# A 31-tap channelwise convolution: one channel tile on TensorE through diagonal weights, or two through shifted copies made by way of DRAM

## The chip, the core and the metric

The kernel runs on one core of a Trainium2 chip. The metric is the time that the device takes for one execution, in microseconds (us), lower being better. TensorE (PE in the profile), VectorE (DVE), ScalarE (ACT) and GpSimd (POOL) compute; SyncE (SP) only issues DMAs.

## The reference, cut to what matters

Two layers of a decoder trunk on 256 tokens of 1024 features, in float32. Layer 0 is attention of two kinds and a gated feed-forward; layer 1 is a gated MLP (mixer C) beside a convolution (mixer D), and a second feed-forward. The change lies in mixer D:

```python
proj = h @ w_in + b_in
gz, ca, cg = jnp.split(proj, [2 * GMLP_WIDTH, 2 * GMLP_WIDTH + CONV_CH], axis=-1)
gu, gv = jnp.split(jax.nn.gelu(gz), 2, axis=-1)
... # mixer C: layer norm of gv, a causal 128 x 128 product per group, times gu
c = ca * jax.nn.sigmoid(cg)
c = lax.conv_general_dilated(c, conv_w[:, None, :], window_strides=(1,), padding=[(CONV_KERNEL - 1, 0)],
                             dimension_numbers=('NWC', 'WIO', 'NWC'), feature_group_count=CONV_CH) + conv_b
d_out = jax.nn.silu(layer_norm(c, cln_g, cln_b))
return jnp.concatenate([c_out, d_out], axis=-1) @ w_out
```

`c` has 512 channels and 256 tokens. Each channel has 31 weights of its own, and its output at token s is the sum over t of weight t times the input at s + t - 30.

## The kernel before

Activations lie with channels on the partitions: 512 channels are four tiles (`ct` 0 to 3) of 128. Every large product is made of float32r parts: weights and activations are split into a high and a low part, and three products (`passes`, L225 to L227, high-high, high-low, low-high) give one of nearly float32 accuracy. Weights come in blocks of 1 MB on SP's queue (`Block.load`, L116) into a ring of three buffers `raw`. ScalarE makes each half's high part `whi` (L133), and VectorE, or GpSimd for some blocks, the low part `wlo` (L137). When a block's second half is split, the load of the block three places on is issued, so that this load waits for that split. The order of TensorE is that of the code, and GpSimd's in this stage too; the other engines and SP are ordered by a scheduler when the program is built.

`tick` is called once or twice per group of products. It spreads two kinds of background work over the stage: splitting of later weight blocks (`pump`), and taps of the convolution on VectorE (`taps_along`, `TAP_RATE` taps per tick).

In layer 1 the stage around the change runs so on TensorE (L1137 to L1162): `gated(0)` makes channel tiles 0 and 1 of `c` into `cpad` (30 zeros ahead of 256 tokens), `gv_steps(1)`, `gated(1)` (tiles 2 and 3), `project_gu(0)`, 12 taps of tile 3, `project_gu(1)`, four products `spatial(p)` of mixer C with two taps behind each, and the last 11 taps. Tiles 0 to 2 are convolved on VectorE: a tap is one scalar_tensor_tensor (L1077, the first one L1075) over 128 channels and 256 tokens. Tile 3 is convolved on TensorE (`taps_pe`, L1056): each tap has a diagonal 128 x 128 matrix, high and low part, which ScalarE makes from the identity (`tap_diag`, L929, twelve of them while layer 0's feed-forward runs, 19 in this stage), and three products with the split tile `c_hi`, `c_lo`.

After that: `spatial(p)` (L1122) ends in a chain of ScalarE, GpSimd twice, ScalarE, GpSimd (L1131 to L1135) that writes part p of `oT_hi`, `oT_lo`. The output projection `out_steps` (L1207) begins with three steps of three products (`SOME[0]`): part 0 for both halves of the output columns, then part 1 for the first half. Then `mean` (L1170) sums the four convolved tiles over channels, and `center`, `scale`, `conv_out` make the layer norm and write parts 4 to 7. The rest is the residual, a norm, and layer 1's feed-forward (blocks `f1`, loaded from `in_ffn_w_in`).

Of the kernel before, what the change touches and what calls it, by code (L numbers as in the profile page):

```python
# [28 lines left out]
P = 128  # L29
# [7 lines left out]
EPS = 1e-6  # L37
NEG = -3.0e38
TAPS = 31


WRAW = 3
# [20 lines left out]
N_T1 = (10, 5, 10)  # L63


TAP_RATE = 0.55
N_DIAG = 12
SOME = (3, 4, 2, 4)
LAMBDA_INIT = 0.8 - 0.6 * math.exp(-0.3 * 0)

# [2 lines left out]
def trunk_kernel(ctx: ExitStack, tc: tile.TileContext, a: dict, out: bass.AP):  # L73
# [4 lines left out]
    wsplit = ctx.enter_context(tc.tile_pool(name="wsplit", bufs=8))  # L78
    act = ctx.enter_context(tc.tile_pool(name="act", bufs=1))
    small = ctx.enter_context(tc.tile_pool(name="small", bufs=3))  # L80
    pmm = ctx.enter_context(tc.tile_pool(name="pmm", bufs=4, space=bass.MemoryType.PSUM))

    def mm_bank():
# [195 lines left out]
    def col(name, i):  # L279
        return vec[:, rows[name] + i:rows[name] + i + 1]  # L280
# [62 lines left out]
    def run(steps):  # L343
        for _ in steps:
            pass
# [572 lines left out]
    wsT = mp.tile([P, NH, P], F32, name="wsT")  # L918
    biasT = mp.tile([P, 4, P], F32, name="biasT")
    cw = mp.tile([P, TAPS, 4], F32, name="cw")  # L920
    cw2 = mp.tile([P, 2, TAPS * 4], F32, name="cw2")
    bv = mp.tile([P, 512], F32, name="bv")
    ones = mp.tile([P, P], F32, name="ones")
    diag = mp.tile([P, N_DIAG, 2, P], FR, name="diag")

    def tap_diag(d, t, ct):

        for i in range(2):
            nc.scalar.activation(d[:, i, :], ident, AF.Copy, scale=cw2[:, i, t * 4 + ct:t * 4 + ct + 1])  # L929

    def odd_setup(ptag):

# [44 lines left out]
        nc.tensor.transpose(pt[:, :TAPS * 4], cw_rows[:TAPS * 4, :P], ident[:TAPS * 4, :TAPS * 4])  # L977
        cwf = cw.rearrange("p a b -> p (a b)")
        nc.vector.tensor_copy(cwf, pt[:, :TAPS * 4])
        hi = mp.tile([P, TAPS * 4], FR, name="cw_hi")  # L980
        nc.scalar.activation(hi, cwf, AF.Copy)
        nc.vector.tensor_copy(cw2[:, 0, :], hi.bitcast(F32))
        nc.vector.tensor_tensor(cw2[:, 1, :], cwf, hi.bitcast(F32), op=ALU.subtract)
        for t in range(N_DIAG):
            tap_diag(diag[:, t], t, 3)
        yield

    with tc.tile_pool(name="ffn0", bufs=1) as fp, tc.tile_pool(name="pf0", bufs=1, space=bass.MemoryType.PSUM) as pf:
# [12 lines left out]
    with tc.tile_pool(name="odd", bufs=1) as op, tc.tile_pool(name="pod", bufs=1, space=bass.MemoryType.PSUM) as pod:  # L1001
# [45 lines left out]

        follow(gv_steps(0), spare)

        cpad = op.tile([P, 4, S + TAPS - 1], F32, name="cpad")  # L1050
        nc.gpsimd.memset(cpad[:, :, :TAPS - 1], 0.0)
        conv = op.tile([P, 4, S], F32, name="conv")
        c_hi = op.tile([P, S + TAPS - 1], FR, name="c_hi")
        c_lo = op.tile([P, S + TAPS - 1], FR, name="c_lo")

        def taps_pe(ct):  # L1056

            ps = mm_bank()
            for t in range(TAPS):
                d = diag[:, t] if t < N_DIAG else diag2[:, t - N_DIAG]  # L1060
                passes(ps[:, :S], (d[:, 0, :], d[:, 1, :]), (c_hi[:, t:t + S], c_lo[:, t:t + S]), t == 0, t == TAPS - 1)
                if t < TAPS - 1:
                    yield
            nc.vector.tensor_scalar(conv[:, ct, :], ps[:, :S], col("conv_b", ct), None, op0=ALU.add)

        live, credit = deque(), [0.0]
# [24 lines left out]
        def gated(j):  # L1091
            wa, wg = blocks["ca", j], blocks["cg", j]
            for f in range(2):
                ps = mm_bank()
                project_T(ps, 0, wg, f)
                project_T(ps, 1, wa, f)
                ct = 2 * j + f
                sgm = scratch()[:, :S]
                with tc.high_priority(30):
                    sigmoid = nc.scalar.activation(sgm, ps[:, :S], AF.Sigmoid, bias=col("b_in", 12 + ct))  # L1100
                    nc.vector.scalar_tensor_tensor(cpad[:, ct, TAPS - 1:], ps[:, S:], col("b_in", 8 + ct), sgm,
                                                   op0=ALU.add, op1=ALU.mult)
                    if ct == 3:
                        split(c_hi, c_lo, cpad[:, ct, :])
                    else:
                        live.append((ct, 0))
            return sigmoid
# [28 lines left out]

        pool_order = in_order("Pool")  # L1137
        gated(0)
        diag2 = op.tile([P, TAPS - N_DIAG, 2, P], FR, name="diag2")
        for t in range(N_DIAG, TAPS):  # L1140
            tap_diag(diag2[:, t - N_DIAG], t, 3)
        run(gv_steps(1))
        last = gated(1)
        with tc.issue_after(last.ins):
            for m in range(MT):
                gv_stats(m)
        project_gu(0)
        taps = taps_pe(3)
        for _ in range(N_DIAG):
            next(taps)  # L1150
        for m in range(MT):
            gv_norm(m)
        last = project_gu(1)
        with tc.issue_after(last.ins):

            nc.scalar.activation(small.tile([P, 2], F32, name="st2")[:, 0:1], ident[:, 0:1], AF.Silu)
        for p in range(4):
            spatial(p)
            for _ in range(2):
                next(taps)  # L1160
        run(taps)
        while live:  # L1162
            tap_dve()
        background.clear()
# [3 lines left out]
        cm = [None] * MT  # L1168

        def mean():  # L1170
            for i, ct in enumerate((3, 0, 1, 2)):
                nc.tensor.matmul(pm[:, :S], ones, conv[:, ct, :], start=i == 0, stop=i == 3)

        def center(m):
# [125 lines left out]
```

## Time and profile before

| | |
|---|---|
| median of 3 runs | 631.92 us (630.7 to 632.24) |
| the profiled execution: its time, its span | 633.2 us, 631.4 us |
| TensorE busy, VectorE busy | 609.0 us (96%), 421.1 us (67%) |
| ScalarE busy, GpSimd busy | 345.7 us (55%), 121.7 us (19%) |
| mean granted TensorE clock | 0.989 of full speed |
| DMA | 104.32 MB, mean 165 GB/s |

The span runs from the first to the last instruction. A busy time sums over stages with different limits, so the stage of the convolution, about 355 to 412 us from the start, has to be read by itself: from windows, the engines' timelines and the chain of waits.

### The profile page before, as it was taken

How to read it: one execution, taken by the hardware profiler on the slowest of the kernel's cores; microseconds unless marked ns; L12 is line 12 of the kernel's file. 1: busy time of each engine (PE TensorE's matmuls, PEld its weight loads, DVE VectorE, ACT ScalarE, POOL GpSimd, SP SyncE). 2: the span in 40 equal slices, each digit the busy share in tenths (PEclk: the TensorE clock that was granted, in tenths of full speed). 3: DMA queues.
4: the chain of work that ended last, by engine and by line, in shares of the span. 5: the costliest groups of instructions: out<-in, count | busy, mean ns of one | idle time of the engine just before them, and what ended most of it. 6: DMA issues, size and time to landing. Idle time of an engine off the chain costs nothing.

```text
span 631.4 us, 8906 instructions
## 1 busy us (share of the span) xinstructions
PE 609.0 (96%) x3420; PEld 517.6 (82%) x3420; DVE 421.1 (67%) x710; ACT 345.7 (55%) x621; POOL 121.7 (19%) x97
## 2 busy tenths in 40 slices
PE   7989799999999999999998999988999999999997
PEld 5867577787988888888886899867988888888886
DVE  3799998547666648664446389986766666665431
ACT  5764686555655587553446775446455555554320
POOL 1998321101000000000003695550000000000000
PEclk9999799999999999999999799999999999999999
DMA  7855424224766437555552553225656555555401
GB/s 248 308 196 175 158 106 132 70 66 149 245 225 215 146 128 266 185 168 185 199 197 67 167 199 134 68 89 178 208 193 201 196 174 173 193 199 190 145 0 67
DMA packets 72791, 104.32 MB, mean 165 GB/s; under 512 B 3068, under 2 KB 56492, under 8 KB 72748
## 3 DMA queue, kind: packets, MB, share of 16 engines
q1 hardware_dynamic: 72748, 103.74, 49.5%
q8 instruction: 27, 0.44, 0.3%
q14 instruction: 16, 0.13, 0.1%
HBM read 102.69 MB, written 1.05 MB: 164 GB/s over the span
## 4 chain that ended last, share of the span: by engine, by line
PE 52%; issue 29%; DVE 11%; POOL 3%; ACT 2%; DMA 1%; SPq 1%; POOLq 0%; DVEq 0%; ACTq 0%
PE mm L233 15%; PE mm L225 8%; PE mm L227 8%; PE mm L234 8%; PE mm L226 8%; DVE wlo L137 3%; DVE scr L331 2%; PE tq L700 1%; DMA raw<-in_even_w_in 1%; POOL rm L310 1%; DVE t L627 1%; PE po L728 1%; ACT whi L133 1%; DVE t L621 1%; PE tq L718 1%
## 5 line engine op out<-in xcount | busy, mean ns | idle before, releaser
L133 ACT ACTIVATE whi<-raw 128x1024 fp32r<-128x1024 f32 (+1 forms) x192 | 197.7, 1040 | 175.7 <-PE mm L233 80.1
L137 DVE TENSOR_TENSOR wlo<-raw,whi 128x1024 fp32r<-128x1024 f32 (+1 forms) x166 | 206.3, 1248 | 124.5 <-ACT whi L133 122.9
L233 PE MATMUL mm<-xT,whi 128*128 128x512 f32 x640 | 226.8, 399 | 0.0
L234 PE MATMUL mm<-xT,wlo 128*128 128x256 f32 x640 | 179.7, 281 | 0.0
L233 PEld LDWEIGHTS mm<-xT,whi 128*128 128x128 f32 x640 | 120.2, 188 | 29.6 <-issue 0.2
L234 PEld LDWEIGHTS mm<-xT,wlo 128*128 128x128 f32 x640 | 120.9, 189 | 0.0
L225 PE MATMUL mm<-whi,xT 128*128 128x512 f32 (+1 forms) x176 | 68.2, 387 | 0.6 <-ACT xT L545 0.5
L137 POOL TENSOR_TENSOR wlo<-raw,whi 128x1024 fp32r<-128x1024 f32 (+1 forms) x26 | 62.9, 2439 | 19.7 <-ACT whi L133 19.6
L227 PE MATMUL mm<-whi,hT_lo 128*128 128x512 f32 (+1 forms) x176 | 66.5, 378 | 0.0
L226 PE MATMUL mm<-wlo,hT_hi 128*128 128x512 f32 (+1 forms) x176 | 66.5, 378 | 0.0
L225 PE MATMUL mm<-whi,hT_hi 128*128 128x512 f32 (+1 forms) x176 | 66.4, 378 | 0.0
L227 PE MATMUL mm<-whi,xT 128*128 128x512 f32 (+1 forms) x176 | 64.1, 364 | 1.1 <-DVE xT L240 1.1
L226 PE MATMUL mm<-wlo,xT 128*128 128x512 f32 (+1 forms) x176 | 64.3, 366 | 0.5 <-DVE wlo L137 0.5
L310 POOL TENSOR_TENSOR rm<-st,neg_half 128x1 f32<-128x1 f32 x8 | 7.1, 894 | 188.9 <-DVE st L308 188.9
L225 PEld LDWEIGHTS mm<-whi,xT 128*128 128x128 f32 x176 | 34.5, 196 | 7.8 <-issue 1.6
L227 PEld LDWEIGHTS mm<-whi,xT 128*128 128x128 f32 x176 | 34.6, 196 | 6.8 <-DVE xT L240 1.8
L226 PEld LDWEIGHTS mm<-wlo,xT 128*128 128x128 f32 x176 | 34.7, 197 | 4.8 <-DVE wlo L137 1.3
L225 PEld LDWEIGHTS mm<-whi,hT_hi 128*128 128x128 f32 x176 | 33.1, 188 | 6.4
L226 PEld LDWEIGHTS mm<-wlo,hT_hi 128*128 128x128 f32 x176 | 33.1, 188 | 6.4
L227 PEld LDWEIGHTS mm<-whi,hT_lo 128*128 128x128 f32 x176 | 33.0, 188 | 6.4
L464 DVE TENSOR_TENSOR scr<-mm,scr 128x256 f32<-128x256 f32 x80 | 33.2, 418 | 5.8 <-ACT scr L463 5.7
L1077 DVE SCALAR_TENSOR_TENSOR cv<-cpad,cw,cv 128x256 f32<-128x256 f32 x87 | 35.7, 481 | 0.2
(226 smaller groups left out, 868.6 us busy)
## 6 DMA issues: line engine op xcount, KB each, us to landing
raw<-in_ffn_w_in SPq DMA_DIRECT2D x44, 1024.0 KB
raw<-in_ffn_w_out SPq DMA_DIRECT2D x22, 1024.0 KB
raw<-in_even_w_in SPq DMA_DIRECT2D x10, 1024.0 KB
raw<-in_odd_w_in SPq DMA_DIRECT2D x8, 1024.0 KB
raw<-in_even_w_out SPq DMA_DIRECT2D x4, 1024.0 KB
raw<-in_odd_w_out SPq DMA_DIRECT2D x4, 1024.0 KB
xs<-in_x SPq DMA_DIRECT2D x4, 256.0 KB
raw<-in_even_w_in SPq DMA_DIRECT2D x4, 256.0 KB
```

The costliest lines, as they stand in the source:

```text
L133: nc.scalar.activation(self.half(f)[0][:, r], self.source(f)[:, r], AF.Copy)
L137: self.lo_engine.tensor_tensor(lo[:, r], self.source(f)[:, r], hi[:, r].bitcast(F32), op=ALU.subtract)
L225: nc.tensor.matmul(ps, lhs[0], rhs[0], start=first, stop=False)
L226: nc.tensor.matmul(ps, lhs[0], rhs[1], start=False, stop=False)
L227: nc.tensor.matmul(ps, lhs[1], rhs[0], start=False, stop=last)
L233: nc.tensor.matmul(bank, w[0], x[2][:, k, :, :].rearrange("p a b -> p (a b)"), start=k == 0, stop=False)
L234: nc.tensor.matmul(bank[:, :S], w[1], x[0][:, k, :], start=False, stop=k == KT - 1)
L310: nc.gpsimd.tensor_tensor(r, t[:, 1:2], neg_half[:, :1], op=ALU.pow)
L331: nc.vector.scalar_tensor_tensor(xn[n], xs[:, m, n * 512:(n + 1) * 512], r, gB[:, n * 512:(n + 1) * 512], op0=ALU.mult, op1=ALU.mult)
L464: nc.vector.tensor_tensor(s, bank[:, :S], s, op=ALU.add)
L621: nc.vector.scalar_tensor_tensor(t1v, psv, rx[m], c, op0=ALU.mult, op1=ALU.mult)
L1077: nc.vector.scalar_tensor_tensor(conv[:, ct, :] if t == TAPS - 1 else acc, cpad[:, ct, t:t + S], cw[:, t, ct:ct + 1], acc, op0=ALU.mult, o ...
```

## The change

Two channel tiles (2 and 3) instead of one go to TensorE, in another form; tiles 0 and 1 stay on VectorE. A product now has a contraction over 128 rows that are four taps times 32 channels, and 32 output columns. Its weights are `W4`, four small diagonal blocks above each other, made once during layer 0's feed-forward: eight small loads of `conv_w`, a transpose, and eight multiplications on GpSimd. Its input is `shifted`: for group g of 32 channels, row 32 j + c holds channel c's tokens moved by j places. A tile needs 8 groups of taps times 4 groups of channels, 32 products, plain float32, each with its own 32 columns of the array and its own 32 rows of PSUM. The copies are made by five DMAs per tile on SP's queue: `cpad` goes to DRAM (`rows`), and four reads bring it back, each moved by one more token (`sh`).

```diff
-TAP_RATE = 0.55
-N_DIAG = 12
+ON_PE = (2, 3)
+TAP_RATE = 0.65
...
+    dr = ctx.enter_context(tc.tile_pool(name="dr", bufs=1, space=bass.MemoryType.DRAM))
...
-    cw2 = mp.tile([P, 2, TAPS * 4], F32, name="cw2")
-    diag = mp.tile([P, N_DIAG, 2, P], FR, name="diag")
-
-    def tap_diag(d, t, ct):
-
-        for i in range(2):
-            nc.scalar.activation(d[:, i, :], ident, AF.Copy, scale=cw2[:, i, t * 4 + ct:t * 4 + ct + 1])
+
+    NQ = 4 * len(ON_PE)
+    TG = -(-TAPS // 4)
+    w4 = mp.tile([P, TG, NQ], F32, name="w4")
+    W4 = mp.tile([P, NQ, TG, 32], F32, name="W4")
...
-        for t in range(N_DIAG):
-            tap_diag(diag[:, t], t, 3)
+        rows4 = scratch()
+        nc.gpsimd.memset(rows4[:NQ * TG, :P], 0.0)
+        src = a["conv_w"][0]
+        for t in range(TG):
+            n = min(4, TAPS - 4 * t)
+            nc.sync.dma_start(rows4[t * NQ:(t + 1) * NQ, :n * 32].rearrange("p (a b) -> p a b", b=32),
+                              bass.AP(tensor=src.tensor, offset=src.offset + 4 * t * CH + ON_PE[0] * P,
+                                      ap=[[32, NQ], [CH, n], [1, 32]]))
+        yield
+        pt = ptag()
+        nc.tensor.transpose(pt[:, :NQ * TG], rows4[:NQ * TG, :P], ident[:NQ * TG, :NQ * TG])
+        nc.vector.tensor_copy(w4.rearrange("p a b -> p (a b)"), pt[:, :NQ * TG])
+        same = mp.tile([P, 32], F32, name="same")
+        nc.vector.tensor_reduce(same, ident.rearrange("p (a b) -> p b a", b=32), axis=AX.X, op=ALU.add)
+        for q in range(NQ):
+            nc.gpsimd.tensor_tensor(W4[:, q], same[:, None, :].to_broadcast([P, TG, 32]),
+                                    w4[:, :, q, None].to_broadcast([P, TG, 32]), op=ALU.mult)
...
-        c_hi = op.tile([P, S + TAPS - 1], FR, name="c_hi")
-        c_lo = op.tile([P, S + TAPS - 1], FR, name="c_lo")
+        NX = S + 4 * (TG - 1)
+        shifted = {ct: op.tile([P, 4, NX], F32, name=f"sh{ct}") for ct in ON_PE}
+
+        rows_d = {ct: dr.tile([P, S + TAPS + 1], F32, name=f"rows{ct}") for ct in ON_PE}
+
+        def shift(ct):
+
+            nc.sync.dma_start(rows_d[ct], cpad[:, ct, :])
+            pitch = S + TAPS + 1
+            for j in range(4):
+                nc.sync.dma_start(shifted[ct][32 * j:32 * j + 32, :, :],
+                                  bass.AP(tensor=rows_d[ct].tensor, offset=rows_d[ct].offset + j,
+                                          ap=[[pitch, 32], [32 * pitch, 4], [1, NX]]))
 
         def taps_pe(ct):
 
             ps = mm_bank()
-            for t in range(TAPS):
-                d = diag[:, t] if t < N_DIAG else diag2[:, t - N_DIAG]
-                passes(ps[:, :S], (d[:, 0, :], d[:, 1, :]), (c_hi[:, t:t + S], c_lo[:, t:t + S]), t == 0, t == TAPS - 1)
-                if t < TAPS - 1:
-                    yield
+            q0 = 4 * (ct - ON_PE[0])
+            for t in range(TG):
+                for g in range(4):
+                    nc.tensor.matmul(ps[32 * g:32 * g + 32, :S], W4[:, q0 + g, t, :], shifted[ct][:, g, 4 * t:4 * t + S],
+                                     start=t == 0, stop=t == TG - 1)
+                tick(1)
             nc.vector.tensor_scalar(conv[:, ct, :], ps[:, :S], col("conv_b", ct), None, op0=ALU.add)
...
-                    if ct == 3:
-                        split(c_hi, c_lo, cpad[:, ct, :])
+                    if ct in ON_PE:
+                        shift(ct)
                     else:
                         live.append((ct, 0))
...
         project_gu(0)
-        taps = taps_pe(3)
-        for _ in range(N_DIAG):
-            next(taps)
         for m in range(MT):
             gv_norm(m)
         last = project_gu(1)
...
+        for ct in ON_PE:
+            taps_pe(ct)
         for p in range(4):
             spatial(p)
-            for _ in range(2):
-                next(taps)
-        run(taps)
         while live:
             tap_dve()
...
-            for i, ct in enumerate((3, 0, 1, 2)):
+            for i, ct in enumerate((2, 3, 0, 1)):
                 nc.tensor.matmul(pm[:, :S], ones, conv[:, ct, :], start=i == 0, stop=i == 3)
```

What stands in SP's queue around the copies. Before, from the last loads of layer 1's first weights to the first feed-forward:

```order
L321 DMA gB<-in_ffn_norm_g 128x1024
L116 DMA raw<-in_odd_w_in 128x8x256 x3
L116 DMA raw<-in_odd_w_out 128x2x1024 x4
L116 DMA raw<-in_ffn_w_in 128x8x256 x22
L116 DMA raw<-in_ffn_w_out 128x2x1024 x11
```

And now (`sh_3349` and `rows_3351` are tile 2's copies, `sh_3350` and `rows_3352` tile 3's):

```order
L323 DMA gB<-in_ffn_norm_g 128x1024
L118 DMA raw<-in_odd_w_in 128x8x256 x3
L118 DMA raw<-in_odd_w_out 128x2x1024 x4
L1072 DMA rows_3351<-cpad 128x288
L1075 DMA sh_3349<-rows_3351 32x4x284 x4
L1072 DMA rows_3352<-cpad 128x288
L118 DMA raw<-in_ffn_w_in 128x8x256
L1075 DMA sh_3350<-rows_3352 32x4x284 x4
L118 DMA raw<-in_ffn_w_in 128x8x256 x21
```

Tile 2's copies stand behind the four loads of `in_odd_w_out`; the reads of tile 3's copies stand behind the first load of `in_ffn_w_in` as well.

On TensorE, the end of `project_gu(1)` and what follows. Before:

```order
L225 MATMUL mm<-xT,whi 128x256
L226 MATMUL mm<-xT,whi 128x256
L227 MATMUL mm<-xT,wlo 128x256
L1127 MATMUL tq<-wsT,gn 64x128 x4
L225 MATMUL mm<-c_hi,diag_3501 128x256
L226 MATMUL mm<-c_lo,diag_3501 128x256
L227 MATMUL mm<-c_hi,diag_3501 128x256
```

And now:

```order
L228 MATMUL mm<-xT,whi 128x256
L229 MATMUL mm<-xT,wlo 128x256
L1085 MATMUL mm<-sh_3349,W_1602 32x256 x32
L1085 MATMUL mm<-sh_3350,W_1602 32x256 x32
L1151 MATMUL tq<-wsT,gn 64x128 x4
L1151 MATMUL mm<-wsT,gn 64x128 x4
L1151 MATMUL tq<-wsT,gn 64x128 x4
L1151 MATMUL mm<-wsT,gn 64x128 x4
L227 MATMUL mm<-whi,oT_hi 128x512
```

The products of both tiles now stand ahead of all four `spatial`, which follow each other without taps between them.

On VectorE, the end of the convolution and the centring. Before:

```order
L1064 TENSOR_SCALAR conv<-mm,vec 128x256
L1077 SCALAR_TENSOR_TENSOR cv_3307<-cpad,cw,cv_3307 128x256
L1077 SCALAR_TENSOR_TENSOR cv_3308<-cpad,cw,cv_3308 128x256
L1077 SCALAR_TENSOR_TENSOR conv<-cpad,cw,cv_3306 128x256
L1077 SCALAR_TENSOR_TENSOR conv<-cpad,cw,cv_3307 128x256
L1077 SCALAR_TENSOR_TENSOR conv<-cpad,cw,cv_3308 128x256
L137 TENSOR_TENSOR wlo<-raw,whi 128x1024
L1177 SCALAR_TENSOR_TENSOR scr<-tq,conv 128x512
L137 TENSOR_TENSOR wlo<-raw,whi 128x1024
L1182 TENSOR_REDUCE scr<-scr 128x128
```

And now:

```order
L1101 SCALAR_TENSOR_TENSOR conv<-cpad,cw,cv_3303 128x256
L1101 SCALAR_TENSOR_TENSOR conv<-cpad,cw,cv_3304 128x256
L139 TENSOR_TENSOR wlo<-raw,whi 128x1024 x2
L1088 TENSOR_SCALAR conv<-mm,vec 128x256 x2
L1194 SCALAR_TENSOR_TENSOR scr<-tq,conv 128x512
L1199 TENSOR_REDUCE scr<-scr 128x128
```

VectorE's own taps now end ahead of the two `conv` that it takes from TensorE, and no weight split is left between the two instructions of the centring.

## Rows read from the trace of the kernel before

**Rows 1.** Windows: busy time of each engine (x instructions), granted clock, DMA share, GB/s

```profile
380.00:400.00 20.00, 20.00 (x173) 19.39 (x172) 18.92 (x45) 10.37 (x16) 9.20 (x6) 1.00 0.42 150
```

**Rows 2.** Chain of waits, in order of time: start, us, what

```profile
411.05 1.49 DVE wlo L137
412.54 0.60 DVE scr L1177
```

**Rows 3.** Timeline of TensorE: start, us (of the whole row), line, tile, count

```profile
387.68 0.28 PE L225 MATMUL mm<-c_hi,diag 128*128 128x256 f32 x1
...
391.94 0.28 PE L225 MATMUL mm<-xT,whi 128*128 128x256 f32 x1
...
397.79 0.66 PE L1127 MATMUL tq<-wsT,gn 128*64 128x128 f32 x8
...
401.55 0.66 PE L1127 MATMUL tq<-wsT,gn 128*64 128x128 f32 x8 [0.69 <-ACT scr L1131]
...
410.47 1.89 PE L1172 MATMUL tq<-conv,ones 128*128 128x256 f32 x8
```

**Rows 4.** Groups of L1172 and L1127: ns min/median/max, first and last start

```profile
L1172 PE MATMUL tq<-conv,ones x8: 377/379/379, 410.5 to 412.0; 128*128 128x256 f32 x8
...
L1127 PE MATMUL tq<-wsT,gn x16: 272/273/324, 397.8 to 401.9; 128*64 128x128 f32 x16
```

**Rows 5.** Window of L1127 alone: PE and PEld, with instructions in flight

```profile
397.87:397.93 0.06, 0.06 (x2) 0.06 (x4) 1.00 0.70 239
```

**Rows 6.** Timeline of SP's queue: start, us to issue

```profile
365.91 0.37 SPq L116 DMA_DIRECT2D raw<-in_odd_w_in  x1
383.25 0.37 SPq L116 DMA_DIRECT2D raw<-in_odd_w_out  x1
396.12 0.37 SPq L116 DMA_DIRECT2D raw<-in_ffn_w_in  x1
628.65 0.33 SPq L1251 DMA_DIRECT2D out<-xs  x1
```

**Rows 7.** Waits of SP's queue: us in total, times, longest

```profile
SPq L1295 <- DMA out<-xs: 1.3, 1, 1.3
```

**Rows 8.** Timeline of ScalarE, with idle time before and its releaser

```profile
371.27 2.01 ACT L133 ACTIVATE whi<-raw 128x1024 fp32r<-128x1024 f32 x2 [1.45 <-DMA raw<-in_odd_w_in]
...
401.04 0.46 ACT L1131 ACTIVATE scr<-tq,vec 128x256 f32<-128x256 f32 x1
...
402.25 0.47 ACT L1131 ACTIVATE scr<-tq,vec 128x256 f32<-128x256 f32 x1 [0.39 <-PE tq L1127]
```

**Rows 9.** Window while one 1 MB load moves

```profile
399.00:400.00 1.00, 1.00 (x13) 0.69 (x12) 1.00 (x3) 0.99 (x3) 0.00 (x0) 1.00 1.09 377
```

**Rows 10.** Timeline of GpSimd

```profile
391.15 4.94 POOL L137 TENSOR_TENSOR wlo<-raw,whi 128x1024 fp32r<-128x1024 f32 x2
...
406.43 0.74 POOL L1135 TENSOR_TENSOR oT_lo<-scr,oT_hi 128x256 fp32r<-128x256 f32 x1 [0.53 <-ACT oT_hi L1134]
```

**Rows 11.** Timeline of VectorE

```profile
386.07 0.44 DVE L240 TENSOR_TENSOR c_lo<-cpad,c_hi 128x286 fp32r<-128x286 f32 x1
...
393.75 14.19 DVE L1077 SCALAR_TENSOR_TENSOR cv<-cpad,cw,cv 128x256 f32<-128x256 f32 x36
```

**Rows 12.** Windows around two idle stretches of TensorE

```profile
345.05:347.70 2.65, 0.00 (x0) 0.00 (x0) 2.65 (x2) 1.30 (x5) 2.65 (x2) 0.97 0.00 0
347.70:354.40 6.70, 6.29 (x23) 5.21 (x24) 4.66 (x4) 3.95 (x12) 4.95 (x2) 0.50 0.39 110
...
425.27:427.20 1.93, 0.00 (x0) 0.00 (x1) 1.93 (x4) 0.72 (x3) 0.00 (x0) 1.00 1.01 347
427.20:430.00 2.80, 2.80 (x12) 2.35 (x13) 1.81 (x2) 2.56 (x5) 0.00 (x0) 1.00 1.08 358
```

**Rows 13.** Window of layer 0's feed-forward

```profile
200.00:250.00 50.00, 50.00 (x296) 43.28 (x295) 33.97 (x51) 34.47 (x69) 0.93 (x1) 1.00 0.56 178
```

**Rows 14.** Group of L929: count, ns min/median/max, first and last start

```profile
L929 ACT ACTIVATE diag<-ident,cw x62: 384/388/403, 225.4 to 367.5; 128x128 fp32r<-128x128 f32 x62
```

More of the change, by code (lines that the diff above doesn't have):

```diff
@@ L39 @@
 TAPS = 31
+CH = 512
 WRAW = 3
@@ L979, in odd_setup @@
         nc.vector.tensor_copy(cwf, pt[:, :TAPS * 4])
[L980 to L983, printed above, removed]
-        for t in range(N_DIAG):
-            tap_diag(diag[:, t], t, 3)
+        rows4 = scratch()
[15 more added lines that the diff above has]
+                                    w4[:, :, q, None].to_broadcast([P, TG, 32]), op=ALU.mult)
         yield
@@ L1048, in trunk_kernel @@
         follow(gv_steps(0), spare)
-        cpad = op.tile([P, 4, S + TAPS - 1], F32, name="cpad")
+        cpad = op.tile([P, 4, S + TAPS + 1], F32, name="cpad")
         nc.gpsimd.memset(cpad[:, :, :TAPS - 1], 0.0)
+        nc.gpsimd.memset(cpad[:, :, S + TAPS - 1:], 0.0)
         conv = op.tile([P, 4, S], F32, name="conv")
-        c_hi = op.tile([P, S + TAPS - 1], FR, name="c_hi")
-        c_lo = op.tile([P, S + TAPS - 1], FR, name="c_lo")
+        NX = S + 4 * (TG - 1)
[8 more added lines that the diff above has]
+                                          ap=[[pitch, 32], [32 * pitch, 4], [1, NX]]))
         def taps_pe(ct):
             ps = mm_bank()
-            for t in range(TAPS):
-                d = diag[:, t] if t < N_DIAG else diag2[:, t - N_DIAG]
-                passes(ps[:, :S], (d[:, 0, :], d[:, 1, :]), (c_hi[:, t:t + S], c_lo[:, t:t + S]), t == 0, t == TAPS - 1)
-                if t < TAPS - 1:
-                    yield
+            q0 = 4 * (ct - ON_PE[0])
[4 more added lines that the diff above has]
+                tick(1)
             nc.vector.tensor_scalar(conv[:, ct, :], ps[:, :S], col("conv_b", ct), None, op0=ALU.add)
@@ L1100, in gated @@
                     sigmoid = nc.scalar.activation(sgm, ps[:, :S], AF.Sigmoid, bias=col("b_in", 12 + ct))
-                    nc.vector.scalar_tensor_tensor(cpad[:, ct, TAPS - 1:], ps[:, S:], col("b_in", 8 + ct), sgm,
+                    nc.vector.scalar_tensor_tensor(cpad[:, ct, TAPS - 1:S + TAPS - 1], ps[:, S:], col("b_in", 8 + ct), sgm,
                                                    op0=ALU.add, op1=ALU.mult)
-                    if ct == 3:
-                        split(c_hi, c_lo, cpad[:, ct, :])
+                    if ct in ON_PE:
+                        shift(ct)
                     else:
@@ L1138, in trunk_kernel @@
         gated(0)
-        diag2 = op.tile([P, TAPS - N_DIAG, 2, P], FR, name="diag2")
-        for t in range(N_DIAG, TAPS):
-            tap_diag(diag2[:, t - N_DIAG], t, 3)
         run(gv_steps(1))
```

## The prediction, made before the changed kernel was run

> **What bounds the kernel now.** I read the windows first. In the 20 us ahead of the end of the convolution TensorE is busy for all 20.00 us, VectorE for 18.92 [rows 1]. So TensorE's own instruction order sets the time here, and what it is given or spared counts, until it has to wait. Then the chain of waits at the place where the stage ends: it runs over a weight split and the centring on VectorE, with TensorE's sum over channels (`mean`) just ahead [rows 2, 3]. So the question is when `mean` may start. TensorE's timeline gives the dates: 12 taps from 387.68, `gu(1)` from 391.94 to 397.79, the first `spatial` at 397.79, `mean` at 410.47 [rows 3]. All times below are in the clock of the old trace.
>
> **What goes from TensorE.** The 36 products of the 12 taps took 391.94 - 387.68 = 4.26 us [rows 3]. `gu(1)` now ends at 397.79 - 4.26 = 393.5. The other 19 taps between and behind the `spatial` (57 products) go too.
>
> **What comes: the products.** Plain float32 leaves two records per product in the trace: `mean`, four products, has eight, each 0.38 us long from start to end and overlapping the next, 1.89 us in all: one starts (1.89 - 0.38) / 7 = 0.215 us after the other [rows 3, 4]. One product over 256 tokens is 0.43 us, 32 of them one after the other 13.76 us. Do four column groups run side by side? The only rows with column groups are `spatial`'s, two groups of 64. Eight records of 128 tokens take (0.66 - 0.27) / 7 = 0.055 us each [rows 3, 4], half of 0.215 / 2 = 0.107, the price by the token when they run alone. In a window inside them two products are in flight throughout, and four weight loads [rows 5]. So two groups overlap fully, and their loads cost nothing seen. Bounds for a tile of 32 products: 3.44 us (four at a time), 6.88 (two), 13.76 (one). I take 3.44, since the row shows the full factor for the groups that it has, and keep the others as rivals.
>
> A rule speaks against that. The Trainium skill ("TensorE: Matmul & The Clock Gate", section "Packing small matmuls — row/col tiling") says that a weight load overlaps products in flight only where its group of rows differs, and gives 3.07 times for four packed tiles. Here all 128 rows are used by every product. By an estimate from that page a tile would take 13.76 / 3.07 = 4.5 us, and the sum would be 1.05 us higher. The window [rows 5] shows loads in flight beside products that use the same 128 rows, so I follow the row.
>
> **What comes: the copies.** They stand in SP's queue, which issues in order. Tile 2: the store and four reads stand behind the load of `in_odd_w_out` issued at 383.25 [rows 6]. A 1 MB load needs 5.3 us from issue to use: issued 365.91 [rows 6], released ScalarE at 371.27 [rows 8]. So it is there at 388.5. The store (0.147 MB) adds 0.4 us by the 377 GB/s of a window in which a load moves [rows 9]. The reads wait for the store's end and are issued within 1.1 us more (three further issues at 0.37 [rows 6]). One small DMA, the output's, took 0.33 us to issue and 1.3 us of waiting for its end [rows 6, 7]; with the step between I estimate 1.85. Reads landed, at such a price: about 391.8, before TensorE asks at 393.5. Hidden by 1.7 us. The products end at 393.5 + 3.44 = 396.9.
>
> Tile 3: its reads stand behind the first load of `in_ffn_w_in`. That one was issued at 396.12 [rows 6], since it waits for the split that GpSimd makes from 391.15 for 4.94 us [rows 10], behind the norm of `gv` on VectorE. VectorE's order now has one tap fewer ahead of that norm (14.19 / 36 = 0.39 us) and no `c_lo` (0.44, part of it in a pause) [rows 11]: I take 0.75 us, so 395.4. The load is there at 400.7. The four reads (0.58 MB) are issued by 396.9 and move behind it: 0.58 / 0.377 = 1.5 us [rows 9], landed about 402.2. So TensorE, done with tile 2 at 396.9, waits 5.3 us for tile 3. All `spatial` stand behind those products and wait too.
>
> After such a wait the clock falls. TensorE idle for 2.65 us and then at work had 0.50, the level of 1.2 GHz, for 6.7 us; after 1.93 us of idle time it had 1.00 [rows 12]. At 5.3 us I expect the fall: the first stretch of tile 3 runs at half speed, and `spatial` perhaps. Bounds: nothing, or 3.44 us (all of it at half speed). I take 2.4, as part of the low stretch passes within the wait. Tile 3 ends, and `spatial` starts, at 402.2 + 3.44 + 2.4 = 408.0.
>
> **From there to `mean`.** `mean` stands behind three steps of the output projection, the third of which needs part 1 of `oT_lo`. The chain of `spatial` gives it. From TensorE's start to ScalarE's is 402.25 - 401.55 = 0.70 us [rows 3, 8]; from ScalarE's start on part 0 (401.04 [rows 8]) to the end of part 1 on GpSimd (406.43 + 0.74 [rows 10]) is 6.13. The last product ahead of `mean` adds 0.23. Sum 7.06. Before, `spatial` began at 397.79, early enough to be hidden by taps: now nothing lies beside it. `mean` starts at 408.0 + 7.06 = 415.1, and started at 410.47 [rows 3]: +4.6.
>
> **Behind `mean`.** A weight split of 1.49 us stood between the mean and the centring on VectorE [rows 2]; VectorE's taps no longer fill its queue to the end, so this split runs earlier. The mean ends at 410.47 + 1.89 = 412.36 [rows 3], the centring began at 412.54 [rows 2]: -0.2. The sum: 4.6 - 0.2 = +4.4 us.
>
> **Edits at nothing.** ScalarE loses 62 diagonal weights of 0.388 us, 24 us [rows 14]; TensorE had no idle time there and waited for none. VectorE loses 28 taps of 0.39, 11 us [rows 11]: the gain would be real only if VectorE were last, and now TensorE is. The new weights `W4` (eight products on GpSimd, of about the size of its 0.74 us one [rows 10], eight small loads at 0.37 us on SP [rows 6], a transpose) are made while TensorE is busy 50.00 of 50 us and GpSimd 0.93 [rows 13]. If that cover were gone: at most 8 x 0.74 + 8 x 0.37, 8.9 us one after the other; if the relief of ScalarE helped, TensorE has nothing left to gain in that window. I take 0, with 0 to 2 us in the range, as the splits there have slack.
>
> **Forecast.** The profiled execution took 633.2 us, its span 631.4 (1.8 around it). 633.2 + 4.4 = 637.6. The median of the runs shown, 631.92, is 1.3 below the profiled execution, so 636.3 on that footing. Its own range: 634.0 (half the clock's price, reads 1 us earlier, and 0.3 smaller) to 639.5 (full price of the clock, reads 1 us later, W4 1 us). Chance 0.52.
>
> **Rivals**, on the same footing.
> 1. Tile 3's reads don't stand behind the 1 MB load but run beside it, by their own 1.85 us after 396.9: landed 398.8. The wait is 1.9 us, at which the clock stays. Tile 3 ends 402.2, `mean` 409.3: -1.2, with -0.2: 630.5. For it: they are other bytes, and 16 engines share them. Against it: the same queue, and the window shows these engines full [rows 9]. Chance 0.12.
> 2. The other side: the reads are there almost when tile 2 is done, by 396.9, because the load and they are issued earlier (GpSimd's split starts earlier when VectorE has fewer taps ahead). Tile 3 ends 400.3, `mean` 407.4: -3.1 - 0.2, so 628.6, faster. It decides once the copies of tile 3 land before 400.0 at full clock: then `mean` is at 400.0 + 3.44 + 7.06 = 410.5, as before. Chance 0.08.
> 3. Only two column groups run side by side. Tile 2 lasts from 393.5 to 400.4, the wait shrinks to 1.8, the clock stays, tile 3 ends 409.1, `mean` 416.2: +5.7 - 0.2, so 637.4. For it: no row shows more than two. Against it: nothing in the row hints at a limit. Chance 0.13.
> 4. The reads go to 32 partitions each and move at half the rate: 3.1 us, landed 403.8: +1.6, so 637.9. No row shows a read into 32 partitions. Chance 0.10.
> 5. No overlap at all, 13.76 us a tile: 393.5 to 407.3, 421.0, `mean` 428.1: +17.6 - 0.2, 649.3. Against it: [rows 5]. Chance 0.05.
>
> On rival 1, the Trainium skill ("DMA: Bandwidth & Descriptors", section "Queues, rings and completion order") says that each engine takes the descriptors of one queue in the order of its ring; by it the reads wait for the load and 636.3 stands. No row shows a small DMA behind a large one.
>
> **How the numbers follow.** Predicted: the likeliest, 636.3. A measurement of this kernel tells 0.3%, some 1.9 us, from no change: 630.0 to 633.8 counts as the same. Rival 2 and a part of rival 1 are faster (0.11), the rest of rival 1 and the low edge of the forecast the same (0.12), all else slower (0.77). Range: from 630.4, the time of rival 1, below which rival 2 lies (0.08), to 643.0: the forecast's upper end 639.5 with a tile on TensorE 1 us dearer for each of the two tiles and 1.5 us of the W4 bound left; above it is rival 5 (0.05).
>
> **What would show it.** Right: in the trace after, the first product with `sh` of tile 2 follows `gu(1)` at once, near 393.5; 32 products take 3.4 us; TensorE then waits about 5 us, released by the DMA of tile 3's copies; the granted clock is at 0.50 for a stretch behind it; `spatial` starts near 408, and `mean` 7.1 us later. Wrong: four products at a time not in flight (windows of that line), the first wait at tile 2 and not at tile 3, no wait at all, or a chain of waits that runs over VectorE's taps. What would break the forecast most is the place of tile 3's reads behind the 1 MB load: if they land before it, the change costs nothing.

## The result, and the profile after

| | before | changed |
|---|---|---|
| median (4 runs each, same chip) | 632.08 us (630.7 to 632.71) | 642.96 us (640.56 to 643.67) |
| ratio, 95% interval | | 1.0173 (1.0149 to 1.0197) |
| span of the profiled execution | 631.4 us | 641.6 us |

Slower, as forecast, but by 10.9 us where 4.4 were forecast. 641.6 - 631.4 = 10.2 us of it can be followed in the two profiled executions, each of them slower than the median of its kernel.

First the windows of the changed kernel, with the columns of [rows 1]. TensorE was busy for all of the 20 us from 380 to 400; now for 18.68, and behind that for nothing at all:

```profile
380.00:400.00 20.00, 18.68 (x190) 16.86 (x189) 18.56 (x43) 11.99 (x16) 10.29 (x6) 1.00 0.58 180
...
399.00:400.00 1.00, 0.00 (x0) 0.00 (x0) 1.00 (x2) 0.00 (x0) 0.00 (x0) 1.00 1.08 385
...
402.00:404.50 2.50, 0.00 (x0) 0.00 (x0) 0.00 (x0) 0.00 (x0) 0.00 (x0) 0.50 1.09 225
...
406.00:407.00 1.00, 1.00 (x16) 0.54 (x12) 0.00 (x0) 0.00 (x0) 0.00 (x0) 0.50 1.02 326
...
408.00:409.00 1.00, 1.00 (x24) 0.67 (x20) 0.00 (x0) 0.00 (x0) 0.00 (x0) 0.91 0.00 0
```

From 402 to 404.5 no engine works and the DMA engines are full, but move 225 GB/s where the load at 399 moved 385: all wait for tile 3's copies. The granted clock (third value from the end) is then at 0.50, and still is at 407.

TensorE's timeline of the changed kernel answers to [rows 3]: both tiles, the first `spatial`, `mean`.

```profile
395.02 3.66 PE L1085 MATMUL mm<-sh,W 128*32 128x256 f32 x64
...
405.03 5.19 PE L1085 MATMUL mm<-sh,W 128*32 128x256 f32 x64 [6.35 <-DMA sh<-rows]
410.15 0.66 PE L1151 MATMUL tq<-wsT,gn 128*64 128x128 f32 x8
...
417.34 1.89 PE L1189 MATMUL tq<-conv,ones 128*128 128x256 f32 x8
```

Tile 2 does not wait, tile 3 waits 6.35 us, and `mean` is 417.34 - 410.47 = 6.9 us later than in [rows 3]. SP's queue (against [rows 6]) shows why: tile 3's reads are issued behind the load of 396.86.

```profile
384.79 0.50 SPq L1072 DMA_DIRECT2D rows<-cpad  x1
389.97 1.76 SPq L1075 DMA_DIRECT2D sh<-rows  x4
391.83 0.38 SPq L1072 DMA_DIRECT2D rows<-cpad  x1
396.86 0.40 SPq L118 DMA_DIRECT2D raw<-in_ffn_w_in  x1
397.35 1.98 SPq L1075 DMA_DIRECT2D sh<-rows  x4
```

Then the chain of waits (start, us, what). In [rows 2] it ran over a weight split to the centring. Now it runs over the copies, the products, and then all four parts of `spatial`: ScalarE, GpSimd, GpSimd, ScalarE, GpSimd, and again. The rows of the parts between are left out.

```profile
398.89 6.00 DMA sh<-rows
...
405.03 5.19 PE mm L1085 x64
...
410.86 0.48 ACT scr L1155
...
411.41 0.74 POOL scr L1156
...
420.49 0.74 POOL scr L1157
...
421.25 0.02 ACT oT_hi L1158
...
421.58 0.62 ACT scr L1197
...
422.29 1.04 DVE scr L1199
...
434.86 0.61 DVE oT_lo L242
```

The step to see is 421.25 to 421.58: ScalarE's square for the centring (L1197) stands in its order behind the last part of `spatial`. What it squares was ready 1.6 us earlier, at 419.27 + 0.69 = 419.96, on VectorE:

```profile
419.27 0.69 DVE L1194 SCALAR_TENSOR_TENSOR scr<-tq,conv 128x512 f32<-128x512 f32 x1 [8.50 <-PE tq L1189]
```

Before, the last part of `spatial` was over in time, and the square waited for its own input (ScalarE's timeline):

```profile
411.49 0.42 ACT L1134 ACTIVATE oT_hi<-scr 128x256 fp32r<-128x256 f32 x1 [2.36 <-POOL scr L1133]
413.23 0.64 ACT L1180 ACTIVATE scr<-scr 128x512 f32<-128x512 f32 x1 [1.32 <-DVE scr L1177]
```

What follows `mean` is therefore late by itself, not only because `mean` is.

Last, windows around the pause ahead of the first product that needs the layer norm. [rows 12] show the place before, where the clock stayed at 1.00; the first line here is that pause with the work in it, before, and the two others are the changed kernel:

```profile
424.90:427.20 2.30, 0.37 (x2) 0.00 (x1) 2.30 (x4) 1.09 (x3) 0.00 (x0) 1.00 0.94 307
...
433.16:435.52 2.36, 0.40 (x3) 0.00 (x1) 2.36 (x4) 1.12 (x3) 0.00 (x0) 1.00 0.96 289
435.52:439.20 3.68, 3.68 (x9) 2.96 (x10) 2.69 (x3) 2.55 (x5) 0.00 (x0) 0.54 1.07 355
```

Nine products were done in 3.68 us at 0.54; before, at 1.00, twelve in 2.80 us [rows 12].

So the 10.2 us are: `mean` 6.9 later; the first product behind the layer norm 435.52 - 417.34 = 18.2 us after `mean`, before 427.20 - 410.47 = 16.7 [rows 3, 12], 1.5 more; from that product to the end 641.6 - 435.5 = 206.1 us, before 204.2, 1.9 more.

### The profile page after: what moved, and what is told of

Read it like the earlier page. It is cut to its first block, busy times and chain, and to the rows that moved or that the text cites. A ratio compares the mean times of both kernels' runs of the same rounds, so it can differ in the third digit from the quotient of the medians.

```text
span 641.6 us, 8947 instructions
## 1 busy us (share of the span) xinstructions
PE 610.7 (95%) x3456; PEld 513.4 (80%) x3456; DVE 407.9 (64%) x679; ACT 327.9 (51%) x557; POOL 130.6 (20%) x107
## 4 chain that ended last, share of the span: by engine, by line
PE 71%; DVE 10%; issue 8%; POOL 5%; DMA 2%; ACT 2%; SPq 1%; POOLq 0%; ACTq 0%; DVEq 0%
PE mm L235 23%; PE mm L236 12%; PE mm L227 10%; PE mm L229 10%; PE mm L228 10%; DVE wlo L139 2%; PE tq L702 1%; DVE scr L333 1%; DMA raw<-in_even_w_in 1%; POOL wlo L139 1%; DMA sh<-rows 1%; PE mm L1085 1%; DVE t L629 1%; POOL rm L312 1%; PE po L730 1%
## 5 line engine op out<-in xcount | busy, mean ns | idle before, releaser
L466 DVE TENSOR_TENSOR scr<-mm,scr 128x256 f32<-128x256 f32 x80 | 33.4, 417 | 0.0
L711 ACT ACTIVATE e<-sm,nmax 128x128 f32<-128x128 f32 (+1 forms) x48 | 21.3, 446 | 16.3 <-DVE nmax L709 16.3
```

What stands on the lines that cost most here:

```text
L466: nc.vector.tensor_tensor(s, bank[:, :S], s, op=ALU.add)
L711: nc.scalar.activation(e[:, i, b, :kn], sm[:, b, :kn], AF.Exp, bias=nmax[:, q:q + 1], scale=-1.0, accum_out=sums[:, q:q + 1])
```

## The experiments

All times are medians against the kernel before on the same chip, and the kernel before had medians from 629.15 to 632.08 us in these comparisons: kernels are compared by the ratio, of which 0.1% is 0.63 us. Where there is one run, there is no interval.

| run | edit | us | ratio to before |
|---|---|---|---|
| changed kernel | | 642.96 | 1.0173 (1.0149 to 1.0197) |
| e1_align | 32 bytes more ahead of hT | 642.1 | 1.0189 (1.0159 to 1.0219) |
| e2_spatial_first | spatial ahead of both tiles | 633.92 | 1.0054 (1.0029 to 1.0080) |
| e3_reads_first | reads ahead of the load | 635.41 | 1.0091 (1.0059 to 1.0123) |
| e4_before_gap | the kernel before, 32 bytes more | 632.44 | 1.0024 (1.0000 to 1.0048) |
| e5_spatial_and_reads | e1, e2 and e3 | 630.78 | 1.0001 (0.9974 to 1.0028) |
| e6_busy_wait | work during the wait | 639.43 | 1.0123 (1.0072 to 1.0174) |
| e7_unshifted | e3, no shift | 636.08 | one run |
| e8_by_group | e3, 128 partitions a read | 647.22 | one run |
| e9_spatial_between | e1, e3, spatial between the tiles | 630.51 | 0.9988 (0.9967 to 1.0010) |
| e10_both_layers | e9, 32 bytes ahead of layer 1's hT | 629.81 | 0.9983 (0.9965 to 1.0001) |
| e11_spatial_dve | spatial's GpSimd work on VectorE | 636.21 | 1.0092 (1.0066 to 1.0117) |
| e12_one_tile | tile 3 alone on TensorE | 634.31 | 1.0065 (1.0039 to 1.0090) |
| e13_between_dve | e10 and e11 | 627.37 | 0.9932 (0.9908 to 0.9956) |
| e14_group_outer32 | e8, other walk of the source | 634.53 | one run |

My theory after the result had three parts: the wait for tile 3's copies; `spatial`'s chain, which lies beside no other work any more and holds up `mean` and then the centring; and the clock, twice. The rivals were that the wait alone is the loss, and that the copies or the form are dear by themselves.

**The wait, and where it comes from.** e3 holds the load behind the reads:

```
+  copied[0] = read                      # tile 3's last read, in shift()
...
+  with tc.issue_after(copied[0].ins):   # first block of in_ffn_w_in
       nc.sync.dma_start(self.raw[:, rs, :], self.src[:, rs, :])
```

> The changed kernel with the load of the first block of in_ffn_w_in held behind the reads of tile 3's copies in SP's queue; all else in the same order. Theory (order of the queue): the reads are issued about 394 to 396 and landed before TensorE asks at 398.7; no wait, no low clock at the products (3.7 us a tile); spatial starts at 402.4, mean at 409.6, the reduction of the centring at 414.5; the load is hardly later than 396.86. Time 632 to 635, with the low stretch about 435 gone. Rival (the copies are slow by themselves, by their 32 partitions or their shift): the wait remains in part, 2 to 4 us, and the time is 637 to 640.

TensorE's timeline of e3:

```profile
394.50 3.66 PE L1088 MATMUL mm<-sh,W 128*32 128x256 f32 x64
399.44 3.66 PE L1088 MATMUL mm<-sh,W 128*32 128x256 f32 x64 [1.28 <-DMA sh<-rows]
403.03 0.66 PE L1154 MATMUL tq<-wsT,gn 128*64 128x128 f32 x8
...
410.22 1.03 PE L1192 MATMUL tq<-conv,ones 128*128 128x256 f32 x4
```

The wait is 1.28 us instead of 6.35, the clock holds and `mean` starts at 410.22, as before the change. So the order in the queue makes the long wait. But the time, 635.41 us, just above the theory's range, is still 0.9% above the kernel before: `mean` is not where the loss ends. And some wait is left, so the copies are slow themselves. Windows of e3, e7 and e8 while copies move show their rate (the last two columns are DMA share and GB/s):

> The kernel with the reads ahead of the load, and all four reads of a tile take the same tokens: the shift by 1 to 3 tokens is left out, so the convolution is not the reference's. The reads alone moved at 220 to 242 GB/s there, a 1 MB load at 377. Theory (the shift, 4 to 12 bytes off, makes them slow): they move at 350 or more, 1.6 us, and the wait of 1.25 us goes. Rival (32 partitions each make them slow): still 220 to 242.

> The kernel with the reads ahead of the load, and each of a tile's four reads brings one group of channels into all 128 partitions instead of four groups into 32: the same rows of 1136 bytes, the same shifts. Theory (32 partitions each make the reads slow): they move at 350 GB/s or more, and the wait of 1.25 us goes. Rival (the shift, or the rows themselves): still 220 to 242.

```profile
395.00:397.00 2.00, 2.00 (x44) 1.23 (x40) 2.00 (x6) 1.99 (x4) 1.31 (x1) 1.00 0.86 226
```

That is e3; next e7, without the shift:

```profile
395.00:397.00 2.00, 2.00 (x44) 1.23 (x40) 2.00 (x7) 2.00 (x4) 1.13 (x1) 1.00 0.79 238
```

And e8, one group into 128 partitions per read:

```profile
393.00:396.00 3.00, 2.13 (x9) 0.55 (x8) 3.00 (x9) 2.67 (x4) 2.06 (x1) 1.00 0.27 96
```

The shift is not it: 238 GB/s without, 226 with, in one run each. e8 was far slower, at a share of 0.27, which would be about 4 of 16 engines, so it could not answer the question on partitions. In e14 the source is walked by `[[pitch, 32], [1, 4], [1, NX]]` instead of `[[1, 4], [pitch, 32], [1, NX]]`:

> As the kernel whose reads bring one group of channels into all 128 partitions, but the source is walked with the 32 channels outermost and the four shifts inside, so that the rows land in other partitions than the weights are made for (the convolution is not the reference's). Theory (there a read was split over 4 of the 16 DMA engines, share 0.27 at 96 GB/s, because its outermost dimension was 4): with 32 outermost all 16 work, share near 1. If 32 partitions made the first form slow, the rate is then 350 GB/s or more; rival (rows of 1136 bytes, or a source just written): 220 to 240 as in the first form.

The share rose to 0.72 at 214 to 215 GB/s from 390 to 392, and each read took 0.6 to 0.8 us to issue; tile 3's wait was 0.35 us. So the outermost dimension set the share, as the theory says, in one run of each form; into 128 partitions the copies are not faster than 226, though the engines are less full. What holds the first form at 220 to 240 stays open.

**The chain of spatial.** e2 moves the loop over `spatial` ahead of the loop over `taps_pe`, nothing else:

> The changed kernel with the four spatial ahead of the convolution's products on TensorE; the copies stay where they are. Theory (chain): tile 3's copies land as late as before, about 404.9, but the chain of spatial lies beside the wait, so mean follows the products and the three steps of the projection, 410.2 + 2.1 = 412.3 instead of 417.3, and ScalarE no longer has part 3 of spatial ahead of the square (1.2 us more): 636 to 638, and 634 to 636 where the second stretch of low clock goes as well. Rival (the wait and the clock alone are the loss): spatial's chain was hidden, and the time stays within 1 us of 643.

```profile
396.57 0.66 PE L1151 MATMUL tq<-wsT,gn 128*64 128x128 f32 x8 [2.66 <-ACT scr L1155]
...
403.71 3.66 PE L1085 MATMUL mm<-sh,W 128*32 128x256 f32 x64 [2.46 <-DMA sh<-rows]
...
409.51 1.67 PE L1189 MATMUL tq<-conv,ones 128*128 128x256 f32 x7
```

From tile 3 (403.71) to `mean` (409.51) there are only tile 3's products and the three steps of the projection, and no longer `spatial` and its 7.2 us. By the ratios, 1.0173 and 1.0054, 7.5 us of the loss are gone with the copies where they were, a little more than the range said, though the clock still fell behind the norm (the last table below). `spatial` now fills part of the wait, which is 2.46 us, and the clock holds at tile 3. The rival, that `spatial` was hidden and the wait alone is the loss, falls. e11 leaves the order and shortens the chain, by `nc.vector` for `nc.gpsimd` in three lines of `spatial`:

> The changed kernel with the three GpSimd operations of each spatial on VectorE, which is idle there; the copies and the order of TensorE stay. Theory (the chain of spatial, no longer beside other work, is part of the loss): each of the operations takes about 0.4 us instead of 0.74, so from the start of spatial to mean 5 to 6 us instead of 7.2, and part 3 is done 3 to 5 us earlier, so that ScalarE's square no longer waits: 638.5 to 641. Rival (GpSimd's chain was not what mean and the centring waited for): 642 to 643.

Tile 3 still waited (6.53 us) at low clock, but `mean` came 413.14 - 408.14 = 5.0 us after the first `spatial` instead of 7.2, and the time fell to 636.21, below the range I gave. By the ratios about half of the loss, 5.1 us, can be had back with the wait in place. In the traces the short chain is worth 4.0 of that: 2.2 us up to `mean` and 1.8 behind it (the last table). The rest may be a faster pace in layer 1's feed-forward, 261 products in the 45 us from 480 against 257 in the changed kernel, for which the edit gives no reason.

**The clock.** e6 puts 14 products that nobody reads between the tiles:

```
+  busy = mm_bank()
+  for i in range(14):
+      nc.tensor.matmul(busy[:, :S], ones, guT[:, 0, :], start=i == 0, stop=i == 13)
```

> The changed kernel with 14 products more on TensorE between tile 2's and tile 3's, float32, 128 x 256, 0.43 us each, into a bank that nobody reads: TensorE works while it would wait for tile 3's copies. Theory (the wait costs the clock besides its own length): tile 3's products run at 1.00 and take 3.7 us instead of 5.2, so 641.0 to 641.5; if the later low stretches go too, 638. Rival (the clock falls for another reason): tile 3's products still take 5.2 us, and the time is 643 or more.

```profile
395.74 6.31 PE L1178 MATMUL mm<-guT,ones 128*128 128x256 f32 x28
402.48 3.66 PE L1085 MATMUL mm<-sh,W 128*32 128x256 f32 x64 [0.43 <-DMA sh<-rows]
```

With the same wait filled, tile 3 takes 3.66 us instead of 5.19: the low clock after the wait costs 1.5 us here. The second low stretch stayed. The time, 639.43, is lower than this explains, but within its interval of 3 us to either side.

**The layout.** Windows over layer 0's feed-forward, far ahead of the change, showed something that I had no term for: fewer products in the same 45 us at full clock (PE alone; before, changed, e1, e4):

```profile
285.00:330.00 45.00, 45.00 (x200) 1.00 0.58 196
```

```profile
285.00:330.00 45.00, 45.00 (x194) 1.00 0.56 186
```

```profile
285.00:330.00 45.00, 45.00 (x199) 1.00 0.56 192
```

```profile
285.00:330.00 45.00, 45.00 (x195) 1.00 0.56 187
```

The same, from the first to the last start of the products with `hT_hi`, before and changed: 59.9 and 61.5 us, both from 279.2.

```profile
L225 PE MATMUL mm<-whi,hT_hi x88: 389/389/473, 279.2 to 339.1; 128*128 128x512 f32 x88
...
L227 PE MATMUL mm<-whi,hT_hi x88: 389/399/477, 279.2 to 340.7; 128*128 128x512 f32 x88
```

The smaller weights of the new form moved the tiles `hT_hi`, `hT_lo` by 5216 bytes, from multiples of 64 to 32 bytes past one. They are the operand that TensorE loads as weights in these products. e1 and e4 undo it and do it alone, by one unused tile:

```
     W4 = mp.tile([P, NQ, TG, 32], F32, name="W4")
+    gap = mp.tile([P, 8], F32, name="gap")
```

> The changed kernel with an unused tile of 32 bytes per partition behind W4, so that layer 0's hT_hi and hT_lo begin at multiples of 64 bytes again, as in the kernel before (there 174272 and 196800; in the changed kernel 169056 and 191584, 32 bytes off). Order and work are the same. Theory (layout): the products of layer 0's feed-forward with hT, 231 to 237 ns each in the changed kernel, go back to 226 to 227; 252 of them give 1.7 us, so about 641.2. Rival (chance of the run, or more traffic beside them): they stay at 231 to 237 ns and the time at 643.

> The kernel before with an unused tile of 32 bytes per partition behind diag, so that layer 0's hT_hi and hT_lo begin 32 bytes past a multiple of 64. Order and work are the same. Theory (layout): layer 0's 252 products with hT go from 226 to 227 ns to 231 to 237, 1.7 us: 633.6 to 634. Rival: no difference, 632.

The pace follows the address: 199 and 200 products at multiples of 64, 194 and 195 off them. From the first to the last start it is 60.4 us in e1 and 61.4 in e4, so the step costs 1.1 to 1.6 us. (The unused tile moves all that is placed behind it, so that it is the place of `hT` that counts is likely, not shown.) In the whole time it is lost in the spread between runs: e1 is not below the changed kernel, e4's interval begins at 1.0000. Nor is it as large everywhere:

> The kernel with spatial between the tiles and, beside it, an unused tile of 32 bytes per partition ahead of layer 1's hT, which so far begins at 151264 and 173792, 32 bytes past a multiple of 64, in all kernels. Theory (layout): layer 1's products with hT, 228 to 235 ns in the kernel before, go to 226 to 232; 252 of them by 3 to 5 ns give 0.8 to 1.3 us less than without this tile. Rival: the same pace, no difference.

In layer 1 the pace hardly rose with the address: from the first to the last start of these products 59.9 us in e9, 59.6 in e10, and the time is that of e9 within the intervals. What of an address matters is open.

**One tile.** e12 sets `ON_PE = (3,)`:

> The new form for tile 3 alone; tile 2 goes back to VectorE, which has 93 taps again as in the kernel before. Theory: tile 3's copies stand behind no load of in_ffn_w_in and land near 394, TensorE waits at most 1 us, spatial starts near 398, its chain is over before VectorE's taps, and these set mean near 410.5 to 411 as before: 631 to 634. Rival (the form itself, the copies and the DRAM, costs most of the loss): 636 to 640.

```profile
399.62 7.45 DVE cv L1101 x19
407.06 0.40 DVE conv L1101
...
407.50 2.93 PE tq L1189 x6
```

VectorE's taps set `mean` again, as the theory has it, though they ended at 407.5. At 634.31 us, just above the range, the new form for one tile costs 0.65%, and its trace shows where: not in this stage (33.4 us from the end of `gu(1)` to the first product behind the norm, before 33.7 without the 12 taps), but in layer 0's pace (61.5 us from first to last start) and in the clock behind the norm, which fell (0.54). The larger part of the loss comes with the second tile, whose copies stand behind the load.

**Together.** e5, then e9 with the loop of `spatial` between `taps_pe(2)` and `taps_pe(3)`:

> Three of the edits in one: the four spatial ahead of the convolution's products, the load of the first in_ffn_w_in block behind the reads of tile 3's copies, and the 32 bytes that bring layer 0's hT to multiples of 64. Theory (the wait for the copies and the uncovered chain of spatial are the whole loss in this stage): spatial starts near 393, the products follow from 396 to 403.5 with hardly a wait, mean at 405 to 406.5, 4 to 5 us ahead of the kernel before; time 627 to 630. Rival (the centring or the clock behind mean takes it back): mean early, but the first product behind the layer norm no earlier than 427, and the time 631 to 634.

> The changed kernel with tile 2's products first, then the four spatial, then tile 3's products; the load behind the reads, and layer 0's hT at multiples of 64 bytes. Where all spatial stood first, TensorE paused 2.93 us between two of them (ScalarE was still at gelu) and ran at 0.50 for 3 us after. Theory (chain and wait are covered by each other): tile 2's products follow gu(1) near 392.8, spatial from 396.5 to 399, tile 3's to 402.6 without a wait, mean near 404.7, no low clock up to there; behind mean about 217 us to the last product, as before: 625 to 628. Rival (something behind mean sets the end, the splits of the next weights on VectorE): mean early, but the end within 1 us of 630.

Both end at the time of the kernel before, nearer to their rivals than to the theory, though `mean` came at 408.18 and 405.12. In e5 TensorE paused between two `spatial` for ScalarE, 2.65 us. In e9 no wait is left, but its chain shows ScalarE's square behind the last part of `spatial` again, 4 us after the start of `mean`:

```profile
408.99 0.02 ACT oT_hi L1162
...
409.31 0.62 ACT scr L1201
...
410.03 1.04 DVE scr L1203
```

e13 takes this away, with the chain of `spatial` on VectorE:

> The kernel with spatial between the tiles, the load behind the reads and both layers' hT at multiples of 64 bytes, and beside it the three GpSimd operations of each spatial on VectorE, which has no taps left there. There mean came 5 to 8 us ahead of the kernel before, but the last product followed it by 220 us, not 217. Theory (the centring waits on ScalarE behind the last part of spatial, whose chain GpSimd draws out to 11 us): with the short chain mean stays near 402 to 405 and the last product follows it by 217 to 218: 624 to 627, faster than the kernel before. Rival (what is lost behind mean is the clock and the splits of the next weights, whatever spatial does): still 220 us behind mean, 629 to 631.

```profile
402.80 1.74 PE tq L1193 x8
404.57 0.70 DVE scr L1198
...
405.35 0.64 ACT scr L1201
...
406.02 1.08 DVE scr L1203
```

The square follows `mean` at once. 627.37 us, 0.9932 (0.9908 to 0.9956), just above the range: faster than both kernels. The table puts the end of the stage of all these together, from TensorE's timelines, the spans and windows of 3.68 us, one profiled execution each. `gu(1)` ends at 391.0 to 395.0 in them, by what lies ahead of the stage, so `mean` is counted from there (before: from 397.79 - 4.26, without the 12 taps).

| kernel | `gu(1)` ends | `mean`, after that | first product behind the norm, after `mean` | clock from there, 3.68 us | from there to the end |
|---|---|---|---|---|---|
| before | 393.5 | 16.9 | 16.7 | 1.00 | 204.2 |
| changed | 395.0 | 22.3 | 18.2 | 0.54 | 206.1 |
| e3 | 394.5 | 15.7 | 19.2 | 0.65 | 206.0 |
| e6 | 392.2 | 21.1 | 18.1 | 0.57 | 206.1 |
| e9 | 393.5 | 11.6 | 18.1 | 0.54 | 206.0 |
| e2 | 392.8 | 16.7 | 16.5 | 0.55 | 206.0 |
| e5 | 392.5 | 15.6 | 16.5 | 1.00 | 204.3 |
| e11 | 393.1 | 20.0 | 16.3 | 0.54 | 204.2 |
| e13 | 391.0 | 11.7 | 16.3 | 0.58 | 205.6 |

Ahead of the norm's first product the times are near 16.5 where the square does not stand behind the last part of `spatial`, and 18 to 19 where it does; a low clock in the centring is part of that in the changed kernel, e3, e6 and e9, while e1 and e10, with the clock at 1.00 there, need 18.0 and 17.7. The last column is 204.2 to 204.3 where the clock holds behind the norm and about 206 where it falls. e11 is the exception: its clock fell as in the changed kernel, nine products in this window,

```profile
429.48:433.16 3.68, 3.68 (x9) 2.95 (x10) 2.75 (x3) 2.49 (x5) 0.00 (x0) 0.54 1.09 355
```

and its 204.2 comes from the faster pace in layer 1's feed-forward. So the short chain of e11 and e13 did not keep this clock, while e14, with the chain of e3, did: 16 products at 1.00, and 204.5 to the end. What decides it is open.

## Why the prediction was wrong in size

The direction was right, and so was the mechanism up to `mean`: the place of tile 3's reads, the wait, the clock after it and the uncovered chain. The size was not: +4.4 us forecast, +10.9 measured (10.2 between the profiles), mostly because of what stands behind `mean`. By its steps:

- **`gu(1)` ends at 393.5**: 395.0, 1.5 later. Layer 0's products with `hT` start at 279.2 in both profiles and are 1.6 us slower in the changed kernel. I had put the new weights at nothing by the work of making them; that their size moves other tiles I had not thought of.
- **A tile takes 3.44 us**: 3.66 from the first start to the last end, (3.66 - 0.38) / 63 = 0.052 us from record to record, a quarter of 0.215. Four groups overlap fully, at 128 rows each. The rule of the Trainium skill ("TensorE: Matmul & The Clock Gate", "Packing small matmuls — row/col tiling") on weight loads does not hold for these products, and the 3.07 by which I got 4.5 was measured there with four groups of rows, not of columns; the measurement decides.
- **Tile 2's copies are hidden, tile 3's stand behind the load**: right, and e3 shows it. Tile 3's products start at 405.03 instead of 402.2: 1.5 by the late start above (the load was issued at 396.86, not 395.4), 1.4 from the load's issue to TensorE's release. Most of that is the copies' own rate: 0.58 MB at 225 GB/s are 2.6 us, where I took 1.5 at 377. So a rate near my fourth rival's came true, but its reason, the 32 partitions, no run shows. Against the first rival: the reads' packets, told by their 1136 bytes, move from 401.01 to 404.35, the load's, of 1024 bytes, from 397.93 to 401.82. On the order of a ring ("DMA: Bandwidth & Descriptors", "Queues, rings and completion order") this trace agrees with the Trainium skill.
- **The clock falls, 2.4 us**: 1.5 at tile 3, by e6. That I took too much here hid part of the late start, by luck.
- **From spatial to mean 7.06**: 417.34 - 410.15 = 7.19, right.
- **Behind mean -0.2**: +3.3, and this is the step that failed. I followed `spatial` to part 1, which `mean` needs, and stopped there. Parts 2 and 3 go on for 4 us behind the start of `mean`; ScalarE takes the centring's square only after them (421.58), and ahead of the norm's first product the clock fell, where before it held. e2, e11 and e13 give the first back, 1.5 us, by moving or shortening the chain, and e9 keeps it. For the second, 1.9 us in the profiles, I had no term: nine products in 3.68 us, before sixteen. The chain does not decide it (e11, e13 and e14 above), and its cause stays open.
- **VectorE's relief and W4 at nothing**: right for the relief, which is 31 taps (93 before, 62 now) and not 28. VectorE's taps end before 398.5, and then it waits. W4 cost what the first step says.

2.2 us (1.5 + 1.4 - 0.7 at tile 3) came in ahead of `mean` and 3.5 behind it: 4.4 + 5.7 = 10.1.

## What to carry to other kernels

When work that covered a chain is taken away or moved, follow the whole chain that it covered, to its last part, and look at what stands behind that part in each engine's order: the price here was not at the instruction that waited first. Copies for a later step belong ahead of a prefetch in a queue that issues in order, even where they are ready a little later. A change far away can shift the addresses of big operands; count products per window in a stage that should not have changed.

## What the runs showed of the hardware

- Four column groups of 32, each with all 128 rows, ran side by side at full rate: 64 records in 3.66 us, weights changed for each product, 0.052 us from record to record against 0.215 for products of 128 columns.
- A read whose outermost source dimension was 4 moved at 96 GB/s and a DMA share of 0.27 (e8); with 32 outermost 215 GB/s at 0.72 (e14). The Trainium skill has the rule ("DMA: Bandwidth & Descriptors", "Why a DMA increments its semaphore by 16 and not by 1"): the slowest dimensions of source and destination set how many engines a DMA uses; the share agrees.
- The granted clock after a pause is not settled by that pause's length: about the same pause, 2.3 us with 0.4 of work in it, left 1.00 before, in e5 and in e14, and 0.54 after the change.
- Products in layer 0 whose weight operand `hT` lies 32 bytes past a multiple of 64 were 2 to 3% slower (194 and 195 against 199 and 200 in 45 us); in layer 1 the same step of 32 bytes was worth 0.3 us of 60. Other tiles moved with `hT`.
